# An encoder layer on one core: GpSimd left idle until the routing, and the last normalisation rebuilt around PSUM

## The chip, the cores and the metric

One core of a Trainium2 chip runs the kernel. The metric is the device time of one execution in microseconds (us). TensorE is called PE, VectorE DVE, ScalarE ACT, GpSimd POOL; SP is the engine that here only issues transfers.

## The reference, cut to what matters

```python
mod = silu(c) @ w_ada + b_ada                        # 6 vectors: shift, scale, gate, twice
u = x * (1 + sc_a) + sh_a
x = layer_norm(ALPHA * x + g_a * attention_mixer(u), ln1_g, ln1_b)
u = x * (1 + sc_f) + sh_f
x = layer_norm(ALPHA * x + g_f * expert_choice_ffn(u), ln2_g, ln2_b)

def layer_norm(x, g, b):
    mu = mean(x); var = mean((x - mu) ** 2)
    return (x - mu) * rsqrt(var + 1e-5) * g + b

def expert_choice_ffn(u):                            # 16 experts, each takes its 64 best of 512 tokens
    g, idx = top_k(softmax(u @ w_router).T, 64)
    h = silu(u[idx] @ w_gate) * (u[idx] @ w_up)
    return scatter_add((h @ w_down) * g)
```

There are 512 tokens of width 1024, all in f32. The mixer holds 8 heads of latent attention and 4 heads of differential attention; the experts are 2048 wide, so that their weights are 16 x 3 x 8 MB.

## The kernel before

The **front** (about the first 325 us) computes the conditioning vectors, the projections and both attentions, in 32 steps `s`: 16 units of differential attention, then 16 of latent attention. Fillers (projections, latents, their normalisation, the splits below) are woven into the steps. Most products run as three products of a rounded part and a remainder: `split` has ACT write the rounded part and another engine subtract it to get the remainder (line L237). Before, POOL does this subtraction for the normalised latents, the queries and half of `w_ukv`, and in `wo_split` both the multiplication of a block of `w_out` by the gate row (L734) and its subtraction. `wo_split` of the first four blocks stands at steps `W0 + i * WD` = 9, 12, 15, 18; their products (`ga`) begin at step 20. `lat_sums` holds the Newton chain for the norm of the latents (L624 to L168 on the tile `small`); the transposes at L631 wait for it. In this part a scheduler sets the order of the instructions on each engine, from a model of their durations.

The **experts** run in 8 pairs. SP streams the weights through 1 MB pages in a fixed order (`stream`, issued in `prefetch` at L954 whenever a page is free): 16 pages of `w_gate`, 16 of `w_up`, 16 of `w_down` for a pair. In the last pair the second half of `w_down` comes in half pages, first those of output columns 0 to 511 (c = 0), then those of 512 to 1023 (c = 1). `up` multiplies block by block, k = 0 to 7; the last blocks of `w_up` are taken column by column, so that `hidden` (DVE) and `hidden_t` (transposes, L1353) of one column run beside the next.

The **last pair** ends in `down_last`. After each block of c = 1 `finish_first` brings one tile's columns 0 to 511 home: a product that scatters (PE), an addition and the statistics (DVE). `gated(1)` scales the other half, four products scatter it into four banks that hold the residual already (by a product with the identity), and `finish` normalises. It runs two Newton chains on DVE, one for two tiles each, and shares multiplications and additions out to DVE, ACT and POOL. The last norm's weight and bias come as one row (`last_rows`), which `spread` copies to all partitions by products of one row with ones (PE, then ACT and DVE empty the banks).

From the routing to the end the order is the program's own (`manual_schedule`).

Of the kernel before, what the change touches and what calls it, by code (L numbers as in the profile page):

```python
# [11 lines left out]
I32 = mybir.dt.int32  # L12
# [4 lines left out]
P = 128  # L17
# [1 line left out]
D = 1024  # L19
KB = 8  # L20
KEEP = 2
W0, WD = 9, 3
MODS = (1, 2, 3, 4, 5, 6, 7, 8, 9)
NEXP = 16
FF = 2048
# [77 lines left out]
def encoder_layer(ctx: ExitStack, tc: tile.TileContext, xT, x, wadaT, cvec, colp, rowp, rows, cst, pos, posr,  # L103
# [503 lines left out]
    def lat_evac(j, bank):  # L607
        hc, c = pages.get(2)
        hs, s = pages.get(2)
        copy(ACT, c, bank)  # L610
        ACT.activation(s, bank, AF.Square)
        lat[j] = (hc, c, hs, s)
        if j == 1:
            POOL.tensor_tensor(s, s, lat[0][3], op=OP.add)

    def lat_sums(bank):
        one = csb[:, C_ONE:C_ONE + 1]
# [17 lines left out]
    def lat_norm(j, bank):  # L635
        hc, c = lat[j][0], lat[j][1]
        DVE.scalar_tensor_tensor(c, c, cols[:, V_GQ + j:V_GQ + j + 1], bank, op0=OP.mult, op1=OP.mult)
        LN_[j] = split(c, 512, POOL)
        pages.put(hc)

    WK, WQ = {}, {}
# [1 line left out]
    def wk_load():  # L643
        hr, raw = pages.get(4)
        SP.dma_start(raw, w_ukv)
        WK["kh"], WK["k"] = split(raw[:, :512], 512, DVE)
        WK["vh"], WK["v"] = split(raw[:, 512:], 512, POOL)
        pages.put(hr)

    def wq_load(p):  # L650
# [51 lines left out]
    def q_proj(h, bank):  # L702
        hw, w = WQ[h // 2]
        for j in range(2):
            o = j * 256 + (h % 2) * P
            mm3(bank, w[:, o:o + P], LN_[j][1][:, :], j == 0, j == 1)
        if h % 2:
            pages.put(hw)
        hf, f = pages.get(2)
        DVE.tensor_tensor(f, bank, CSQ[h % 2], op=OP.mult)  # L710
        QM[h] = split(f, 512, DVE if h < 0 else POOL)
        pages.put(hf)


# [16 lines left out]

    def wo_split(k):
        hr, raw = WO[k]
        POOL.tensor_tensor(raw, raw, GR["r"], op=OP.mult)  # L734
        WOh[k], WO[k] = split(raw, 1024, POOL)
        pages.put(hr)

    Zh, Z = [], []
# [561 lines left out]
    def last_rows():  # L1300
# [3 lines left out]

    late = {(0, "g", 5): take_xs, (0, "g", 6): take_gate, (0, "g", 7): take_hidden, (0, "u", 4): take_hidden_t,
            (0, "u", 5): take_rows, (0, "d", 2): lambda: take_acc(0), (0, "d", 4): lambda: take_acc(1),
            (1, "g", 0): lambda: pages.put(EP["gbh"]), (NP - 1, "g", 7): last_rows}

    def turn(pr, nm, k, hs):
        put_all(hs)  # L1310
# [5 lines left out]
    def up(pr, nm, banks, between, columns=None):  # L1316
# [4 lines left out]
                r = slice(64 * e, 64 * e + 64)  # L1321
                PE.matmul(banks[c][r], xs[:, k, r], w[e][:, c * 512:(c + 1) * 512], start=k == 0, stop=k == 7)  # L1322

        n = KB if columns is None else KB - 2
        for k in range(n):
            h, w = zip(*(loaded.pop((pr, nm, k, e)) for e in range(2)))
            between(k)
# [62 lines left out]

    LB, TB, YB = HALF[0], HALF[1][:2], HALF[1][2:]

    def finish_first(t):
        scatter(NP - 1, t, 0, TB[t % 2])
        DVE.bn_stats(lst[:, 24 * t:24 * t + 6], acc[t][:, 0:512])

    def finish():
        crit.close()
        with tc.manual_schedule():
            gated(1, YB)  # L1400
            for t in range(4):
                mm(LB[t], OHT[(NP - 1) % 2][:, t * P:(t + 1) * P], EP["YS"][:, 512:], False, True)
            l2 = EP["l2"]
            m2 = mv2[:, 0:8].rearrange("p (t c) -> p t c", c=2)
            va, t1, rs, nb = (lst[:, 20 + 24 * j:24 + 24 * j] for j in range(4))

            def half(t, c):
                src = LB[t] if c else acc[t][:, :512]
                return src, acc[t][:, c * 512:(c + 1) * 512], l2[:, c * 512:(c + 1) * 512], l2[:, D + c * 512:D + (c + 1) * 512]

            def stats(t):
                return [lambda: DVE.bn_stats(lst[:, 24 * t + 6:24 * t + 12], LB[t]),  # L1412
                        lambda: DVE.bn_aggr(mv2[:, 2 * t:2 * t + 2],
                                            lst[:, 24 * t:24 * t + 12].rearrange("p (c s) -> p c s", s=6))]

            def centre(t, c):
                src, a, g, b = half(t, c)
                return lambda: DVE.scalar_tensor_tensor(a, src, mv2[:, 2 * t:2 * t + 1], g, op0=OP.subtract, op1=OP.mult)  # L1418

            def store(t, c):  # L1420
                SP.dma_start(out[t * P:(t + 1) * P, c * 512:(c + 1) * 512], acc[t][:, c * 512:(c + 1) * 512])

            def scaled(t, c):
                src, a, g, b = half(t, c)

                def go():
                    DVE.scalar_tensor_tensor(a, a, rs[:, t:t + 1], b, op0=OP.mult, op1=OP.add)  # L1427
                    store(t, c)
                return go

            def other(t, c, last=POOL):
                src, a, g, b = half(t, c)
                ACT.activation(a, src, AF.Identity, scale=rs[:, t:t + 1], bias=nb[:, t:t + 1])
                POOL.tensor_tensor(a, a, g, op=OP.mult)
                last.tensor_tensor(a, a, b, op=OP.add)

            def newton(t):
                p = slice(t, t + 2)
                return [lambda: DVE.tensor_scalar(va[:, p], m2[:, p, 1], LN_EPS, RS_SCALE, op0=OP.add, op1=OP.mult)] + \
                    rsqrt_steps(rs[:, p], va[:, p], t1[:, p], mv2[:, 8 + t:10 + t].bitcast(I32)) + \  # L1440
                    [lambda: DVE.scalar_tensor_tensor(nb[:, p], m2[:, p, 0], -1.0, rs[:, p], op0=OP.mult, op1=OP.mult)]

            def weave(steps, work):
                for i, step in enumerate(steps):
                    step()
                    if i % 2 and work:
                        work.pop(0)()
                for w in work:
                    w()

            for f in stats(0) + stats(1):
                f()
            weave(newton(0), stats(2) + stats(3) + [centre(0, 0), centre(1, 0)])
            other(0, 1)
            other(1, 1)
            weave(newton(2), [scaled(0, 0), scaled(1, 0), centre(2, 0), centre(2, 1), centre(3, 0)])
            store(0, 1)
            scaled(2, 0)()
            scaled(2, 1)()
            store(1, 1)  # L1460
            scaled(3, 0)()
            other(3, 1, DVE)
            store(3, 1)

    for pr in range(NP):
        G, U = HALF[pr % 2], HALF[1 - pr % 2]

        def in_gate(k, pr=pr, U=U):
            if pr == 0:
                gather(0, U[2:], (k + 2) * (k > 0), min(k + 3, KB))  # L1470
                if k == KB - 1:
                    scat_mats(0, U[2])
            elif 1 <= k <= 4:
                for hf in range(2):
                    scatter(pr - 1, k - 1, hf, U[hf])
# [110 lines left out]
```

## Time and profile before

| | |
|---|---|
| time, median of 3 runs (lowest to highest) | 1303.66 us (1299.6 to 1304.99) |
| the profiled execution | 1303.92 us, its span 1302.1 us |
| busy in the span | PE 1185.2, DVE 373.8, ACT 225.0, POOL 118.7 us |
| mean granted clock of PE | 0.969 |
| moved by DMA | 456.10 MB, mean 350 GB/s |

The span runs from the first to the last instruction; 1.8 us of the time lie outside it. A row of a timeline gives start, duration, engine, line, operation, what is written and read, the shape and the count; brackets hold the idle time of the engine ahead of it and what ended that. A granted clock of 1.00 is 2.4 GHz, 0.50 is 1.2 GHz.

### The profile page before, as it was taken

How to read it: one execution, taken by the hardware profiler on the slowest of the kernel's cores; microseconds unless marked ns; L12 is line 12 of the kernel's file. 1: busy time of each engine (PE TensorE's matmuls, PEld its weight loads, DVE VectorE, ACT ScalarE, POOL GpSimd, SP SyncE). 2: the span in 40 equal slices, each digit the busy share in tenths (PEclk: the TensorE clock that was granted, in tenths of full speed). 3: DMA queues.
4: the chain of work that ended last, by engine and by line, in shares of the span. 5: the costliest groups of instructions: out<-in, count | busy, mean ns of one | idle time of the engine just before them, and what ended most of it. 6: DMA issues, size and time to landing. Idle time of an engine off the chain costs nothing.

```text
span 1302.1 us, 13908 instructions
## 1 busy us (share of the span) xinstructions
PE 1185.2 (91%) x5581; PEld 550.5 (42%) x5581; DVE 373.8 (29%) x793; ACT 225.0 (17%) x464; POOL 118.7 (9%) x79
## 2 busy tenths in 40 slices
PE   8899888999899999998899799879978997998793
PEld 5677556777433433432342243224323432432231
DVE  6798897636301111020110012010101110110107
ACT  3465665542210000000000000000000000000000
POOL 2500532320000500000000000000000000000002
PEclk9899998999999999999999999999998999999987
DMA  9775531374999899999999999999999999999981
GB/s 345 291 231 194 176 138 65 130 283 154 385 385 420 335 422 421 421 421 421 421 422 421 421 422 421 421 421 421 422 421 421 420 421 422 421 422 421 422 304 65
DMA packets 76215, 456.10 MB, mean 350 GB/s; under 512 B 8140, under 2 KB 8524, under 8 KB 28018
## 3 DMA queue, kind: packets, MB, share of 16 engines
q1 hardware_dynamic: 75858, 455.08, 86.3%
q8 instruction: 44, 0.72, 0.2%
q14 instruction: 23, 0.19, 0.0%
q10 hardware_dynamic: 290, 0.10, 0.0%
HBM read 453.04 MB, written 3.95 MB: 351 GB/s over the span
## 4 chain that ended last, share of the span: by engine, by line
DMA 45%; PE 27%; DVE 2%; issue 0%; ACT 0%; SPq 0%; DVEq 0%
DMA pg<-in_w_up_dram 19%; DMA pg<-in_w_gate_dram 15%; PE bk L122 14%; PE bk L1322 11%; DMA pg<-in_w_down_dram 11%; PE bk L1353 1%; DVE pg L1427 0%; DVE pg L1418 0%; DVE small L1192 0%; DVE ohg L1194 0%; DVE lst L1412 0%; DVE lst L162 0%; PE bk L1243 0%; DVE mv L165 0%; PE bk L1271 0%
## 5 line engine op out<-in xcount | busy, mean ns | idle before, releaser
L122 PE MATMUL bk<-pg,pg 128*128 128x512 f32 (+4 forms) x2282 | 530.9, 490 | 13.6 <-POOL pg L423 4.4
L122 PEld LDWEIGHTS bk<-pg,pg 128*64 128x64 f32 (+2 forms) x2282 | 259.7, 163 | 237.5 <-issue 176.3
L1322 PE MATMUL bk<-pg,pg 128*64 128x512 f32 x1024 | 242.8, 609 | 35.1 <-DMA pg<-in_w_up_dram 33.6
L1322 PE MATMUL bk<-pg,xs 128*64 128x512 f32 x1024 | 241.0, 605 | 30.3 <-DMA pg<-in_w_up_dram 30.0
L1322 PEld LDWEIGHTS bk<-pg,pg 128*64 128x64 f32 x1024 | 73.6, 139 | 193.3 <-issue 128.5
L1322 PEld LDWEIGHTS bk<-pg,xs 128*64 128x64 f32 x1024 | 73.3, 138 | 183.0 <-issue 124.3
L1347 DVE TENSOR_TENSOR pg<-pg,bk 128x512 f32<-128x512 f32 x32 | 22.0, 688 | 405.0 <-PE bk L1322 405.0
L144 ACT ACTIVATE pg<-bk 128x512 f32<-128x512 f32 (+1 forms) x105 | 59.3, 583 | 434.2 <-PE bk L1353 353.7
L1226 POOL TENSOR_TENSOR ohg<-ohg,aff 128x512 f32<-128x512 f32 x8 | 8.4, 1049 | 789.5 <-DVE ohg L1225 789.5
L1249 DVE TENSOR_TENSOR pg<-pg,bk 128x512 f32<-128x512 f32 x60 | 41.3, 688 | 124.7 <-PE bk L122 124.4
L122 PEld LDWEIGHTS bk<-ohg,pg 128*128 128x128 f32 x512 | 61.3, 196 | 28.8 <-issue 28.8
L122 PE MATMUL bk<-ohg,pg 128*128 128x128 f32 x512 | 67.9, 286 | 0.5 <-DVE ohg L1225 0.5
L1343 ACT ACTIVATE pg<-bk 128x512 f32<-128x512 f32 x32 | 18.8, 598 | 241.3 <-PE bk L1322 241.3
L137 ACT ACTIVATE pg<-pg 128x512 fp32r<-128x512 f32 (+2 forms) x63 | 42.8, 708 | 26.0 <-DVE pg L710 7.0
L237 POOL TENSOR_TENSOR pg<-pg,pg 128x512 fp32r<-128x512 f32 (+1 forms) x20 | 34.8, 1745 | 91.6 <-ACT pg L137 91.5
L1008 DVE CUSTOM_DVE_ANT_0 pg<-pg,pg 128x1024 f32<-128x1024 f32 x32 | 39.7, 1276 | 2.3 <-DMA pg<-in_wadaT_dram 2.2
L1238 DVE TENSOR_SCALAR xs<-bk,Gc,Bc 128x128 f32<-128x128 f32 x16 | 6.6, 410 | 100.1 <-PE bk L122 100.1
L1238 DVE TENSOR_SCALAR pg<-bk,Gc,Bc 128x128 f32<-128x128 f32 x16 | 6.6, 410 | 97.7 <-PE bk L122 97.7
L122 PE MATMUL bk<-pg 64*128 64x512 f32 (+3 forms) x94 | 30.5, 485 | 3.2 <-DMA pg<-in_cvec_dram 2.2
L1386 DVE TENSOR_TENSOR pg<-bk,pg 128x512 f32<-128x512 f32 x16 | 11.1, 692 | 67.5 <-PE bk L122 67.5
L1353 PEld LDWEIGHTS bk<-csb,pg 128*128 128x128 f32 x128 | 17.8, 209 | 26.1 <-issue 22.8
L218 DVE CUSTOM_DVE_ANT_0 pg<-pg,pg 128x1024 f32<-128x1024 f32 x16 | 25.7, 1640 | 5.7 <-DMA pg<-in_wadaT_dram 5.7
(211 smaller groups left out, 629.4 us busy)
## 6 DMA issues: line engine op xcount, KB each, us to landing
pg<-in_w_gate_dram SPq DMA_DIRECT2D x128, 1024.0 KB, 19.8
pg<-in_w_up_dram SPq DMA_DIRECT2D x128, 1024.0 KB, 19.8
pg<-in_w_down_dram SPq DMA_DIRECT2D x120, 1024.0 KB, 19.8
pg<-in_wadaT_dram SPq DMA_DIRECT2D x16, 1024.0 KB, 7.3
pg<-in_wadaT_dram SPq DMA_DIRECT2D x16, 512.0 KB, 6.2
pg<-in_w_down_dram SPq DMA_DIRECT2D x16, 512.0 KB, 10.8
pg<-bias_d SPq DMA_DIRECT2D x16, 256.0 KB, 4.8
pg<-in_w_out_dram SPq DMA_DIRECT2D x8, 512.0 KB, 3.2
```

The source lines that it names most:

```text
L122: PE.matmul(o, l, r, start=start, stop=stop)
L137: return ACT.activation(dst, src, AF.Copy, scale=scale)
L144: ACT.activation(dst, src, AF.Copy)
L218: DVE.tensor_tensor_reduce(out=w2[:, j], in0=w2[:, j], in1=cs, scale=1.0, scalar=0.0, op0=OP.mult, op1=OP.add, accum_out=modr[:, n:n + 1])
L237: lo_eng.tensor_tensor(lo, src, ff(hi), op=OP.subtract)
L1008: DVE.tensor_tensor_reduce(out=w2[:, j], in0=w2[:, j], in1=cs, scale=1.0, scalar=0.0, op0=OP.mult, op1=OP.add, accum_out=modr[:, n:n + 1])
L1238: DVE.tensor_scalar(xs[:, k, :], src, Gc[:, k:k + 1], Bc[:, k:k + 1], op0=OP.mult, op1=OP.add)
L1249: DVE.tensor_add(acc[t][:, c], acc[t][:, c], bank)
L1322: PE.matmul(banks[c][r], xs[:, k, r], w[e][:, c * 512:(c + 1) * 512], start=k == 0, stop=k == 7)
L1343: ACT.activation(EP["HS"][:, c * 512:(c + 1) * 512], banks[c], AF.Silu)
L1347: DVE.tensor_tensor(s, s, U[c], op=OP.mult)
L1353: PE.transpose(G[c % 2][:, i * P:(i + 1) * P], sj[:, i // 2, i % 2, :], ident)
```

## The change

1. In the front every subtraction and multiplication that POOL did from the latents on (`lat_evac`, `lat_norm`, `wk_load`, `q_proj`, `wo_split`) goes to DVE: 13 instructions of 512 elements for each partition and 16 of 1024. `W0, WD` go from 9, 3 to 15, 1.
2. In `up` only k = 7 is taken column by column, in all pairs; before it was k = 6 and 7.
3. `last_rows` takes its page and issues its transfer one gate stage earlier, and `spread` runs in the last pair's gate stage (ahead of k = 6) and no longer after block 1 of its down stage.
4. `finish_first` multiplies a tile's first half by the norm's weight right after its statistics. `finish` runs one Newton chain for all four tiles. The first half of three tiles is made in PSUM: the identity times the bias, a diagonal matrix of -mean/deviation times the weight, and a diagonal matrix of 1/deviation times the weighted values, which ACT then copies out. The second halves and the last tile's first half end on DVE. POOL has nothing left in it.

```diff
-W0, WD = 9, 3
+W0, WD = 15, 1
...
         if j == 1:
-            POOL.tensor_tensor(s, s, lat[0][3], op=OP.add)
+            DVE.tensor_tensor(s, s, lat[0][3], op=OP.add)
...
-        LN_[j] = split(c, 512, POOL)
+        LN_[j] = split(c, 512, DVE)
...
-        WK["vh"], WK["v"] = split(raw[:, 512:], 512, POOL)
+        WK["vh"], WK["v"] = split(raw[:, 512:], 512, DVE)
...
-        QM[h] = split(f, 512, DVE if h < 0 else POOL)
+        QM[h] = split(f, 512, DVE)
...
-        POOL.tensor_tensor(raw, raw, GR["r"], op=OP.mult)
-        WOh[k], WO[k] = split(raw, 1024, POOL)
+        DVE.tensor_tensor(raw, raw, GR["r"], op=OP.mult)
+        WOh[k], WO[k] = split(raw, 1024, DVE)
...
-            (1, "g", 0): lambda: pages.put(EP["gbh"]), (NP - 1, "g", 7): last_rows}
+            (1, "g", 0): lambda: pages.put(EP["gbh"]), (NP - 2, "d", KB - 1): last_rows}
...
-        n = KB if columns is None else KB - 2
+        n = KB if columns is None else KB - 1
...
     def finish_first(t):
         scatter(NP - 1, t, 0, TB[t % 2])
-        DVE.bn_stats(lst[:, 24 * t:24 * t + 6], acc[t][:, 0:512])
+        a = acc[t][:, :512]
+        DVE.bn_stats(lst[:, 24 * t:24 * t + 6], a)
+        DVE.tensor_tensor(a, a, EP["l2"][:, :512], op=OP.mult)
...
+        bias(0)
+        gated(1, YB)
+        bias(1)
+        for t in range(4):
+            mm(LB[t], OHT[(NP - 1) % 2][:, t * P:(t + 1) * P], EP["YS"][:, 512:], False, True)
+            DVE.bn_stats(lst[:, 24 * t + 6:24 * t + 12], LB[t])
+            DVE.bn_aggr(mv2[:, 2 * t:2 * t + 2], lst[:, 24 * t:24 * t + 12].rearrange("p (c s) -> p c s", s=6))
+        bias(2)
+        bias(3)
+        DVE.tensor_scalar(va, m2[:, :, 1], LN_EPS, RS_SCALE, op0=OP.add, op1=OP.mult)
+        rsqrt(rs, va, t1, mv2[:, 8:12].bitcast(I32))
+        DVE.scalar_tensor_tensor(nb, m2[:, :, 0], -1.0, rs, op0=OP.mult, op1=OP.mult)
+
+        for t in range(4):
+            ACT.activation(diag[:, t], ident, AF.Copy, scale=nb[:, t:t + 1])
+            mm(banks[t], diag[:, t], l2[:, :512], False, t == 3)
+            if t < 3:
+                ACT.activation(diag[:, 4 + t], ident, AF.Copy, scale=rs[:, t:t + 1])
+                mm(banks[t], diag[:, 4 + t], acc[t][:, :512], False, True)
+        for t in range(4):
+            centre(t)
+            scaled(t)
+            if t < 3:
+                ACT.activation(acc[t][:, :512], banks[t], AF.Copy)
+            else:
+                a = acc[t][:, :512]
+                DVE.scalar_tensor_tensor(a, a, rs[:, t:t + 1], banks[t], op0=OP.mult, op1=OP.add)
+            store(t, 0)
...
             elif 1 <= k <= 4:
                 for hf in range(2):
                     scatter(pr - 1, k - 1, hf, U[hf])
+            elif k == 6 and pr == NP - 1:
+                spread(EP["l2"], U[2:], (1.0, 1.0))
...
             if pr == NP - 1:
-                if b == 1:
-                    spread(EP["l2"], TB, (1.0, 1.0))
                 if b >= 2:
```

Here `bias(t)` is the product of the identity with the bias half row into `banks[t]`, `centre` is (value - mean) times the weight from the bank, and `scaled` is that times 1/deviation plus the bias, with the store behind it.

**Order on DVE in the front.** Before, the end of the Newton chain for the latents (tile `small`, 128x8) stands among the softmax instructions of differential attention (L527 reads a score bank `bk`, L537 to L539 combine its two maps):

```order
L166 SCALAR_TENSOR_TENSOR small<-small 128x8
L539 SCALAR_TENSOR_TENSOR pg_129_3057<-pg_129_3057,st 128x512
L162 TENSOR_TENSOR small<-small 128x8
L527 ISA pg_7_110,st<-bk_68,pg_34_271 128x512
L527 ISA st 128x1
L537 RECIPROCAL st<-sts 128x1
L162 TENSOR_TENSOR small<-small 128x8
L538 SCALAR_TENSOR_TENSOR st<-sts,small,st 128x1
L167 SCALAR_TENSOR_TENSOR small<-small 128x8
L539 SCALAR_TENSOR_TENSOR pg_142_3124<-pg_142_3124,st 128x512
L168 SCALAR_TENSOR_TENSOR small<-small 128x8
```

Now the same end of the chain has only small instructions in it:

```order
L166 SCALAR_TENSOR_TENSOR small<-small 128x8
L162 TENSOR_TENSOR small<-small 128x8 x2
L167 SCALAR_TENSOR_TENSOR small<-small 128x8
L537 RECIPROCAL st<-sts 128x1
L168 SCALAR_TENSOR_TENSOR small<-small 128x8
```

A little later in the changed kernel the gate multiplications of `w_out` (L734) and their subtraction (L237) stand between the softmax instructions on DVE, where there was nothing of them:

```order
L527 ISA pg_1_78,st<-bk_67,pg_34_271 128x512
L527 ISA st 128x1
L734 TENSOR_TENSOR pg_206_3446<-pg_206_3446,pg_41_314 128x1024
L537 RECIPROCAL st<-sts 128x1
L167 SCALAR_TENSOR_TENSOR st<-st 128x4
L481 SCALAR_TENSOR_TENSOR pg_144_3178<-bk_69,pg_144_3178 128x512
L527 ISA pg_1_78,st<-bk_68,pg_34_271 128x512
L527 ISA st 128x1
L734 TENSOR_TENSOR pg_212_3478<-pg_212_3478,pg_41_314 128x1024
L538 SCALAR_TENSOR_TENSOR st<-sts,small,st 128x1
L168 SCALAR_TENSOR_TENSOR st<-st 128x4
L237 TENSOR_TENSOR pg_210_3475<-pg_206_3446,pg_210_3475 128x1024
```

So the chain got shorter by its neighbours, and POOL's work on `w_out` went in behind it, with the later steps in the program notwithstanding: the scheduler places these instructions while differential attention still runs.

**Order on PE at the end of the last pair's up stage.** Before, a column (one bank `bk`) takes four weight pages, those of k = 6 and of k = 7; a row is one product:

```order
L1322 MATMUL bk_66<-pg_1063_7456,pg_385_4750 64x512
L1322 MATMUL bk_66<-pg_1064_7458,pg_385_4750 64x512
L1322 MATMUL bk_66<-pg_1068_7470,pg_385_4750 64x512
L1322 MATMUL bk_66<-pg_1071_7484,pg_385_4750 64x512
L1322 MATMUL bk_67<-pg_1063_7456,pg_385_4750 64x512
L1322 MATMUL bk_67<-pg_1064_7458,pg_385_4750 64x512
L1322 MATMUL bk_67<-pg_1068_7470,pg_385_4750 64x512
L1322 MATMUL bk_67<-pg_1071_7484,pg_385_4750 64x512
L1353 MATMUL bk_70<-csb,pg_393_4787 128x128 x4
```

Now k = 6 (pages 1060 and 1063) is through all four banks before the first product that needs k = 7:

```order
L1322 MATMUL bk_68<-pg_1060_7462,pg_381_4746 64x512
L1322 MATMUL bk_68<-pg_1063_7472,pg_381_4746 64x512
L1322 MATMUL bk_69<-pg_1060_7462,pg_381_4746 64x512
L1322 MATMUL bk_69<-pg_1063_7472,pg_381_4746 64x512
L1322 MATMUL bk_66<-pg_1064_7474,pg_381_4746 64x512
L1322 MATMUL bk_66<-pg_1067_7488,pg_381_4746 64x512
L1322 MATMUL bk_67<-pg_1064_7474,pg_381_4746 64x512
L1322 MATMUL bk_67<-pg_1067_7488,pg_381_4746 64x512
L1353 MATMUL bk_70<-csb,pg_389_4783 128x128 x4
```

Six products of k = 6 (columns 1 to 3) moved from behind the arrival of k = 7 to ahead of it.

## Rows read from the trace of the kernel before

**Rows 1.** Stages, by stretch: PE, PEld, DVE, ACT, POOL busy; PEclk; DMA share; GB/s.
```profile
125.00:150.00 25.00, 20.22 (x125) 15.88 (x124) 24.03 (x60) 13.56 (x36) 11.20 (x5) 0.98 0.55 189
150.00:212.00 62.00, 52.39 (x280) 36.68 (x280) 52.59 (x124) 39.29 (x91) 19.29 (x11) 0.93 0.36 125
212.00:290.00 78.00, 76.59 (x518) 59.54 (x516) 42.15 (x71) 41.41 (x91) 25.20 (x12) 0.98 0.47 178
...
455.00:1186.00 731.00, 675.94 (x3030) 249.32 (x3028) 84.06 (x134) 36.40 (x67) 6.30 (x6) 0.99 1.01 421
1186.00:1224.00 38.00, 28.38 (x114) 8.53 (x108) 0.00 (x0) 2.05 (x4) 0.00 (x0) 0.96 1.01 421
```

**Rows 2.** PE timeline of the last pair, from the last weights of the up stage.
```profile
1224.75 4.15 PE L1322 MATMUL bk<-pg,pg 128*64 128x512 f32 x10 [1.42 <-DMA pg<-in_w_up_dram]
...
1234.60 3.65 PE L122 MATMUL bk<-pg,pg 128*64 128x512 f32 x16
...
1242.44 5.29 PE L122 MATMUL bk<-pg,csb 1*128 1x512 f32 x8
1247.66 5.50 PE L122 MATMUL bk<-pg,pg 128*64 128x512 f32 x16
1253.09 1.98 PE L122 MATMUL bk<-pg,csb 128*128 128x512 f32 x4
...
1260.50 22.07 PE L122 MATMUL bk<-pg,pg 128*64 128x512 f32 x80
```

**Rows 3.** Issues of w_down from 1224.5 us on (first and last start), and time to landing.
```profile
L954 SPq DMA_DIRECT2D pg<-in_w_down_dram x17: 327/541/3215, 1224.8 to 1255.5; - x17
...
DMA to landing us min/median/max: 10.4/10.8/19.9
```

**Rows 4.** DVE timeline of the end of the kernel.
```profile
1278.12 0.69 DVE L1386 TENSOR_TENSOR pg<-bk,pg 128x512 f32<-128x512 f32 x1 [0.46 <-PE bk L122]
...
1281.21 0.21 DVE L1413 BATCH_NORM_AGGREGATE mv<-lst 128x2 f32<-128x12 f32 x1
...
1285.06 0.75 DVE L1418 SCALAR_TENSOR_TENSOR pg<-pg,mv,pg 128x512 f32<-128x512 f32 x1
...
1298.34 0.68 DVE L1435 TENSOR_TENSOR pg<-pg,pg 128x512 f32<-128x512 f32 x1
```

**Rows 5.** Waits of PE from 95 to 330 us, the longest.
```profile
PE bk L631 <- DVE small L168: 4.0, 1, 4.0
```

**Rows 6.** POOL's instructions from 90 to 330 us, grouped by line.
```profile
L237 POOL TENSOR_TENSOR pg<-pg,pg 128x512 fp32r<-128x512 f32 (+1 forms) x20 | 34.8, 1745 | 91.6 <-ACT pg L137 91.5
L734 POOL TENSOR_TENSOR pg<-pg,pg 128x1024 f32<-128x1024 f32 x8 | 21.0, 2635 | 11.6 <-DMA pg<-in_w_out_dram 10.3 <-ACT pg L144 1.3
L614 POOL TENSOR_TENSOR pg<-pg,pg 128x512 f32<-128x512 f32 x1 | 1.3, 1283 | 34.4 <-ACT pg L611 34.4
```

**Rows 7.** DVE timeline of the front.
```profile
122.61 1.35 DVE L162 TENSOR_TENSOR st<-st 128x4 f32<-128x4 f32 x2
...
135.65 0.16 DVE L162 TENSOR_TENSOR small<-small 128x8 f32<-128x8 f32 x1
...
138.38 0.74 DVE L539 SCALAR_TENSOR_TENSOR pg<-pg,st 128x512 f32<-128x512 f32 x1
139.04 2.35 DVE L162 TENSOR_TENSOR small<-small 128x8 f32<-128x8 f32 x1
...
142.00 1.76 DVE L162 TENSOR_TENSOR small<-small 128x8 f32<-128x8 f32 x1
...
143.93 2.87 DVE L539 SCALAR_TENSOR_TENSOR pg<-pg,st 128x512 f32<-128x512 f32 x1
146.72 2.30 DVE L168 SCALAR_TENSOR_TENSOR small<-small 128x8 f32<-128x8 f32 x1
...
208.79 2.20 DVE L571 SCALAR_TENSOR_TENSOR pg<-pg,st,rowb 128x128 f32<-128x128 f32 x4
...
214.34 1.22 DVE L1008 CUSTOM_DVE_ANT_0 pg<-pg,pg 128x1024 f32<-128x1024 f32 x1
```

More of the change, by code (lines that the diff above doesn't have):

```diff
@@ L1394, in finish_first @@
         scatter(NP - 1, t, 0, TB[t % 2])
-        DVE.bn_stats(lst[:, 24 * t:24 * t + 6], acc[t][:, 0:512])
+        a = acc[t][:, :512]
+        DVE.bn_stats(lst[:, 24 * t:24 * t + 6], a)
+        DVE.tensor_tensor(a, a, EP["l2"][:, :512], op=OP.mult)
     def finish():
-        crit.close()
[L1399 to L1463, printed above, removed]
@@ new lines, in finish, with bias, store, centre @@
+        l2, diag = EP["l2"], EP["HS"].rearrange("p (i q) -> p i q", q=P)
+        banks = [YB[0], TB[0], TB[1], YB[1]]
+        m2 = mv2[:, 0:8].rearrange("p (t c) -> p t c", c=2)
+        va, t1, rs, nb = (lst[:, 20 + 24 * j:24 + 24 * j] for j in range(4))
+        def bias(t):
+            mm(banks[t], ident, l2[:, D:D + 512], True, False)
+        def store(t, c):
+            SP.dma_start(out[t * P:(t + 1) * P, c * 512:(c + 1) * 512], acc[t][:, c * 512:(c + 1) * 512])
+        def centre(t):
+            DVE.scalar_tensor_tensor(acc[t][:, 512:], LB[t], mv2[:, 2 * t:2 * t + 1], l2[:, 512:D], op0=OP.subtract, op1=OP.mult)
@@ new lines, in scaled @@
+        def scaled(t):
+            a = acc[t][:, 512:]
+            DVE.scalar_tensor_tensor(a, a, rs[:, t:t + 1], l2[:, D + 512:], op0=OP.mult, op1=OP.add)
+            store(t, 1)
+        bias(0)
[5 more added lines that the diff above has]
+            DVE.bn_aggr(mv2[:, 2 * t:2 * t + 2], lst[:, 24 * t:24 * t + 12].rearrange("p (c s) -> p c s", s=6))
```

## The prediction

> **What bounds the kernel now.** I read the stages first [rows 1]. From 455 us to the last pair the DMA share is 1.01 at 421 GB/s: the stream of expert weights has no gap and sets the pace, while PE has slack (675.9 of 731 us). Nothing in the change makes the stream smaller, so only two places can give time: what comes before the stream runs without a gap, and what comes after its last weights. In the front PE should be the bound; it is busy for 76.59 of 78 us from 212 to 290, but only for 20.22 of 25 and 52.39 of 62 before that. There DVE is busy for 24.03 of 25 and 52.59 of 62: differential attention is bound by DVE. A time gained or lost in the front passes through whole, since PE starts the experts and the pages come free from there.
>
> The end is the second view: the timeline of PE in the last pair [rows 2]. From 1224.75 on PE is the bound. The reader should see three things. The up stage still has 10 product halves to do when its last weights arrive, at half the pace (4.15 us for 10, where 16 take 3.65), and more behind them. Then a block of 8, the copying of a row to all partitions, takes 5.29 us, and the 16 after it 5.50. And from 1260.50 all is back to back. Meanwhile the weights have arrived: the last transfer is issued at 1255.5 and lands 10.4 us later, at 1265.9 [rows 3], but the last product ends only at 1278.0, just ahead of `gated(1)` at 1278.12 [rows 4]. PE is 12 us behind the stream here.
>
> **The change, part by part.** The sum is made against the profiled execution, 1303.9 us with a span of 1302.1 (the median shown is 1303.7, so the difference carries over).
>
> *k = 7 alone by columns.* When the last page of `w_up` arrives, PE now has 14 halves left in place of 26. The 12 that went ahead (the order on PE shows them as six products) fill its wait for that page. At 3.65/16 = 0.23 us each that is 2.7 us [rows 2]. PE also ran at half clock after its idle wait: 10 halves took 4.15 in place of 2.3, so 1.9 more if it stays busy there. Bounds 2.7 and 4.6; I take 4.0, because the wait is filled mostly. In the other pairs the stream covers it.
>
> *Spread moved.* 5.29 us leave PE's path, and the clock loss behind them, 5.50 - 3.65 = 1.85 us, goes too [rows 2]: 7.1. It now costs about the same in the gate stage, where PE has 38.00 - 28.38 = 9.6 us of idle time to come before the last page [rows 1]. That covers it; without the cover it would be 7.1 us, less what the weights' arrival allows.
>
> *What is late next.* 4.0 + 7.1 = 11.1 us earlier, PE meets the weights. Block 3 of the down stage has its last page at 1224.8 + 19.9 = 1244.7 [rows 3]. From there PE needs 14 halves of block 3 (3.2), two products with the identity (1.98), 64 halves of c = 0 and 1 (14.6) and three scatter products (half of 1.98 each, 3.0): 1267.5. By the other bound the last page lands at 1265.9 and 8 halves (1.8) follow: 1267.7. Both say that the last product ends at about 1268.0 in place of 1278.0. This term is **-10.0**; it would be -11.1 without the weights, and -6 if PE dropped to half clock for some 8 us while it waits for half pages.
>
> *The tail.* Before, from 1278.0 to the end of the last DVE instruction (1298.34 + 0.68) are 21.0 us, and 3.1 more to the end of the span [rows 4]. Now, from the last product on: the fourth scatter 1.0 (two halves); on DVE addition, statistics and the new multiplication ahead of `gated(1)`, 3 x 0.69 = 2.1; `gated(1)` 0.7; the first product of the other half 1.0; four times statistics and aggregate, 4 x (0.61 + 0.21) = 3.3 (0.69 less the 0.08 by which DVE starts the next one early); eleven small instructions, each 0.16 (a row follows in the front's part) and 0.2 from start to start, 2.2; a diagonal on ACT, 0.3 (an estimate, a quarter of a bank copy with its fixed part); seven products on PE at 1.0, 6.9; the last DVE instruction 0.75; 3.1 as before; and about 0.1 for each of eight changes of engine. Sum 22.2 against 24.1. DVE's own eight instructions at 0.7 (5.6 us) lie beside the products. If the products run at half clock, 6.9 becomes 13.8; PE is idle for about 2 us ahead of them. I take half a step of that kind, 1 us. This term is **-1.0**, bounds -3 and +5.
>
> *The front.* PE's longest wait there is for the Newton chain of the latents, 4.0 us [rows 5]. POOL is busy for 34.8 + 21.0 + 1.3 us in this part [rows 6]. While it runs, some DVE instructions are stretched: a small one of the chain takes 2.35 or 1.76 us in place of 0.16, another 2.30, a combination 2.87 in place of 0.74 [rows 7]. The stretched ones read two operands from SBUF. There are 11 such rows between 122.61 and 208.79, and over all of them the excess is 16.2 us. With POOL silent I expect it gone. Against that stands the added work. Until the eighth row maximum of latent attention (about 212 us before) 9 instructions of 512 and 9 of 1024 elements stand newly on DVE; issued back to back they cost about 0.61 and 1.14 (a row shows 1.22, and the next starts some 0.08 before its end), 15.7 us together. So DVE's load up to there stays as it was, within 1 us. What changes is where the lost time lies: 8.0 us of the stretch were inside the chain, for which PE waited 4.0. The order on DVE shows the chain now short and the work on `w_out` behind it. After 212 DVE has 42.15 of 78 us busy [rows 1]; the rest of the 28 us, some 12, fits in. I take **-3.0**: the wait goes, a little is lost elsewhere. Bounds: -14.4, all of PE's idle time from 125 to 212; and +15.7, if nothing is given back.
>
> [...]
>
> The row's page, taken one gate stage earlier, leaves the stream one page less for some 20 transfers; with 19.9 us from issue to landing at 2.5 us a page the queue is eight deep, so one less costs nothing.
>
> Sum: 1303.9 - 10.0 - 1.0 - 3.0 = 1289.9. I predict **1290 us**.
>
> **The rivals.**
> (a) *The front gains nothing or loses a little.* The scheduler's new order puts 1.2 us instructions between the softmax ones, and each may hold a bank that PE wants. For it: DVE is 96% busy from 125 to 150 [rows 1]. Against it: the stretched rows [rows 7]. With +3 in place of -3: 1296.
> (b) *The diagonal products run at half clock.* For it: PE is idle before them, and the row after the spread shows what that does. Against: the pause is short. 6.9 more, with 1 already in: 1296.
> (c) *DVE becomes the front's bound* (the other side). The stretch is not POOL's doing, so nothing comes back: +15.7 until 212, and of the 12 us after that half reach PE's path, since its softmax waits for the same engine: +21.7 in place of -3. 1303.9 - 11.0 + 21.7 = 1314.6. It decides once the front loses more than 11 us. Against it: rows of the same line, with and without POOL beside them, differ by 2 us.
> (d) *The spread isn't covered in its new place.* PE enters the last pair's up columns late, and 3 to 4 us of the term of 10 are lost: 1293.5.
> (e) *The end does nothing*: with PE earlier, the half pages come later, since their issue hangs on something else. Then only -4 stay: 1300. Against it: the last issue at 1255.5 follows landings, not PE.
>
> **How the numbers follow.** Chances: forecast 0.52, (a) 0.17, (b) 0.09, (c) 0.07, (d) 0.10, (e) 0.05. A measurement can tell about 0.5% from no change, that is below 1297.1 or above 1310.2. Faster are the forecast, (b) and (d) and 60% of (a): 0.81. Slower is (c): 0.07. The rest, 0.12, is the same. The forecast's own range is 1285 to 1294. To leave out no more than 2 in 10, the range goes from 1282 (a front that gives 8 us more) to 1299 (above (a), (b) and (d), short of (e)).
>
> **What would show it.** In the profile after: the wait of L631 for L168 gone, no stretched DVE rows, PE's idle time from 125 to 212 below 14.4; in the last pair no row of one-row products behind block 1, waits of PE for `w_down` pages, and the last product within 3 us of the last landing, not 12; in the tail no POOL, and seven products at 0.43 a half. Wrong would make it: a DVE that is busy throughout the front while PE's waits grow, or diagonal products at 0.86 a half.

## The result, and the profile after

The changed kernel takes 1282.59 us (median of 4 runs, 1282.34 to 1285.97) against 1304.02 for the kernel before on the same chip: a ratio of 0.9848, with a 95% interval from 0.982 to 0.9876. Differences between two changed kernels, below, are of their medians; taken by the ratios to the kernel before they come out the same within 1.3 us. The intervals are 2 to 4 us wide to either side, so that a smaller difference is not clear of the noise by the times alone, and the traces have to bear it. The change makes the kernel faster, by 21 us where 14 were forecast. The profiled execution took 1282.34 us, its span is 1280.5 us (1302.1 before).

I split the 21.6 us by events that both traces have: the start of the first product of the experts (`L1322`) and the landing of the last page of `w_down`. First the instructions of `L1322` in the kernel before, by kind (first and last start within the stretch asked for):

```profile
L1322 PE MATMUL bk<-pg,xs x30: 592/592/644, 342.7 to 350.0; 128*64 128x512 f32 x30
```

The same in the changed kernel:

```profile
L1322 PE MATMUL bk<-pg,xs x64: 592/592/643, 332.5 to 349.6; 128*64 128x512 f32 x64
```

And its last transfers of `w_down` with their time to landing, which answer to [rows 3]:

```profile
L954 SPq DMA_DIRECT2D pg<-in_w_down_dram x16: 539/606/3242, 1215.0 to 1243.7; - x16
...
DMA to landing us min/median/max: 10.5/10.8/15.2
```

| | before | after | difference | predicted |
|---|---|---|---|---|
| start to first product of the experts | 342.7 | 332.5 | -10.2 | -3.0 |
| from there to the last landing | 923.3 | 921.7 | -1.6 | 0 |
| from there to the end of the last product | 12.0 | 2.9 | -9.1 | -10.0 |
| from there to the end of the span | 24.1 | 23.4 | -0.7 | -1.0 |

(The last landing is at 1254.2, 10.5 us behind the issue at 1243.7.)

**The front.** The stages of the changed kernel, with the columns of [rows 1]; the second runs to the ninth row maximum of latent attention, which is taken up further below:

```profile
125.00:150.00 25.00, 25.00 (x151) 18.15 (x150) 22.27 (x75) 15.97 (x39) 0.00 (x0) 1.00 0.52 164
...
125.00:199.79 74.79, 68.57 (x405) 50.19 (x404) 69.97 (x187) 53.02 (x123) 0.00 (x0) 0.98 0.49 169
...
212.00:290.00 78.00, 76.75 (x543) 60.16 (x542) 43.98 (x79) 40.88 (x91) 0.00 (x0) 1.00 0.46 172
...
412.00:422.00 10.00, 10.00 (x51) 6.42 (x50) 1.51 (x3) 1.05 (x2) 9.30 (x4) 0.83 0.92 371
```

PE has no pause from 125 to 150, where it had 4.78 us, and POOL is silent. The longest waits of PE from 95 to 330 us (total, times, longest), which answer to [rows 5]:

```profile
PE bk L122 <- DVE pg L710: 4.3, 2, 3.9
PE bk L122 <- ACT pg L137: 3.3, 2, 2.6
```

The wait of L631 is gone; the longest is now for a query's multiplication (L710), ahead of 199.8 us, and the second for ACT's roundings, behind it. The end of the Newton chain for the latents in the DVE timeline, where [rows 7] have 2.35, 1.76 and 2.30 us:

```profile
129.60 0.16 DVE L162 TENSOR_TENSOR small<-small 128x8 f32<-128x8 f32 x1
...
131.32 0.37 DVE L162 TENSOR_TENSOR small<-small 128x8 f32<-128x8 f32 x2
...
132.11 0.15 DVE L168 SCALAR_TENSOR_TENSOR small<-small 128x8 f32<-128x8 f32 x1
...
132.49 0.75 DVE L539 SCALAR_TENSOR_TENSOR pg<-pg,st 128x512 f32<-128x512 f32 x1
...
199.79 0.68 DVE L870 TENSOR_REDUCE st<-bk 128x1 f32<-128x512 f32 x1
```

No row from 80 to 300 us is stretched any more. The last line is the ninth row maximum of latent attention; before, it starts at 212.34.

**The last pair.** PE's timeline, which answers to [rows 2]:

```profile
1212.48 1.93 PE L1322 MATMUL bk<-pg,pg 128*64 128x512 f32 x6 [1.33 <-DMA pg<-in_w_up_dram]
...
1227.92 3.65 PE L122 MATMUL bk<-pg,pg 128*64 128x512 f32 x14 [0.70 <-DMA pg<-in_w_down_dram]
...
1238.91 19.26 PE L122 MATMUL bk<-pg,pg 128*64 128x512 f32 x72
...
1261.01 3.70 PE L122 MATMUL bk<-pg,pg 128*128 128x512 f32 x8 [1.12 <-DVE pg L1386]
...
1268.37 7.97 PE L122 MATMUL bk<-pg,pg 128*128 128x512 f32 x14 [1.94 <-ACT pg L1434]
```

The one-row products are gone from here, and PE now waits for a page of `w_down` (0.70): it has caught up with the stream. The 72 halves end at 1258.17 with the fourth scatter, so the last product ends about 1.0 earlier, at 1257.1. The last line holds the seven diagonal products in 14 halves; 14 at full clock take 6.28 us (a later row), so the clock fell within them (granted 0.79 over these 7.97 us). DVE's timeline of the end, which answers to [rows 4]:

```profile
1259.66 0.69 DVE L1398 TENSOR_TENSOR pg<-pg,pg 128x512 f32<-128x512 f32 x1
1260.27 0.68 DVE L1386 TENSOR_TENSOR pg<-bk,pg 128x512 f32<-128x512 f32 x1
1262.17 0.70 DVE L1425 BATCH_NORM_STATS2 lst<-bk 128x6 f32<-128x512 f32 x1 [1.22 <-PE bk L122]
...
1267.71 0.16 DVE L1431 SCALAR_TENSOR_TENSOR lst<-mv,lst 128x4 f32<-128x4 f32 x1
...
1276.38 0.75 DVE L1446 SCALAR_TENSOR_TENSOR pg<-pg,lst,bk 128x512 f32<-128x512 f32 x1 [2.71 <-PE bk L122]
```

`gated(1)` (L1386) stands behind 2.1 us of other work, PE waits for it, and at the end DVE waits 2.71 us for the diagonal products.

### The profile page after: what moved, and what is told of

It reads as the page before. It is cut to its first block, busy times and chain, and to the rows that moved or that the text cites. A ratio compares the mean times of both kernels' runs of the same rounds, so it can differ in the third digit from the quotient of the medians.

```text
span 1280.5 us, 13903 instructions
## 1 busy us (share of the span) xinstructions
PE 1181.4 (92%) x5603; PEld 554.0 (43%) x5603; DVE 375.4 (29%) x813; ACT 228.2 (18%) x471; POOL 53.9 (4%) x45
## 4 chain that ended last, share of the span: by engine, by line
PE 37%; DMA 36%; DVE 2%; issue 0%; ACT 0%; SPq 0%; DVEq 0%
PE bk L122 23%; DMA pg<-in_w_up_dram 19%; PE bk L1322 13%; DMA pg<-in_w_down_dram 9%; DMA pg<-in_w_gate_dram 8%; PE bk L1353 0%; PE bk L1243 0%; DVE small L1192 0%; DVE ohg L1194 0%; DVE lst L1425 0%; PE bk L1271 0%; DVE mv L1426 0%; DVE pg L1446 0%; DVE lst L1397 0%; ACT aff L838 0%
## 5 line engine op out<-in xcount | busy, mean ns | idle before, releaser
L122 PE MATMUL bk<-pg,pg 128*128 128x512 f32 (+4 forms) x2296 | 542.2, 488 | 22.9 <-ACT pg L137 7.1
L122 PEld LDWEIGHTS bk<-pg,pg 128*128 128x128 f32 (+2 forms) x2296 | 263.1, 161 | 253.6 <-issue 177.5
L1322 PE MATMUL bk<-pg,pg 128*64 128x512 f32 x1024 | 236.4, 601 | 33.4 <-DMA pg<-in_w_up_dram 28.9
L1322 PE MATMUL bk<-pg,xs 128*64 128x512 f32 x1024 | 234.3, 598 | 29.9 <-DMA pg<-in_w_up_dram 27.2
L1322 PEld LDWEIGHTS bk<-pg,pg 128*64 128x64 f32 x1024 | 73.7, 137 | 185.0 <-issue 124.1
L1322 PEld LDWEIGHTS bk<-pg,xs 128*64 128x64 f32 x1024 | 72.7, 136 | 176.5 <-issue 118.8
L1343 ACT ACTIVATE pg<-bk 128x512 f32<-128x512 f32 x32 | 18.8, 598 | 222.1 <-PE bk L1322 222.1
L137 ACT ACTIVATE pg<-pg 128x512 fp32r<-128x512 f32 (+2 forms) x63 | 42.4, 707 | 21.3 <-DVE pg L896 5.2
L237 DVE TENSOR_TENSOR pg<-pg,pg 128x512 fp32r<-128x512 f32 (+1 forms) x40 | 37.1, 933 | 14.8 <-ACT pg L137 14.6
L1008 DVE CUSTOM_DVE_ANT_0 pg<-pg,pg 128x1024 f32<-128x1024 f32 x32 | 37.9, 1221 | 2.1 <-DMA pg<-in_wadaT_dram 2.0
L1386 DVE TENSOR_TENSOR pg<-bk,pg 128x512 f32<-128x512 f32 x16 | 11.1, 691 | 74.7 <-PE bk L122 74.7
L1353 PEld LDWEIGHTS bk<-csb,pg 128*128 128x128 f32 x128 | 17.8, 209 | 26.5 <-DVE pg L1347 13.5
L218 DVE CUSTOM_DVE_ANT_0 pg<-pg,pg 128x1024 f32<-128x1024 f32 x16 | 24.6, 1574 | 5.7 <-DMA pg<-in_wadaT_dram 5.7
```

The source lines that it names most:

```text
L122: PE.matmul(o, l, r, start=start, stop=stop)
L137: return ACT.activation(dst, src, AF.Copy, scale=scale)
L218: DVE.tensor_tensor_reduce(out=w2[:, j], in0=w2[:, j], in1=cs, scale=1.0, scalar=0.0, op0=OP.mult, op1=OP.add, accum_out=modr[:, n:n + 1])
L237: lo_eng.tensor_tensor(lo, src, ff(hi), op=OP.subtract)
L1008: DVE.tensor_tensor_reduce(out=w2[:, j], in0=w2[:, j], in1=cs, scale=1.0, scalar=0.0, op0=OP.mult, op1=OP.add, accum_out=modr[:, n:n + 1])
L1343: ACT.activation(EP["HS"][:, c * 512:(c + 1) * 512], banks[c], AF.Silu)
```

## The experiments

My theory of the front was that DVE and POOL keep each other from SBUF, so that POOL's silence gives the gain. The rival was that the order gives it: the later steps of `w_out` and the work that the scheduler puts ahead of the chain. Of the end, the theory was the prediction's: PE was late, and the columns and the spread made it so.

**The front alone**: before, with part 1 of the change.

> The kernel before with part 1 alone (POOL's front work to DVE, steps 15, 1); the end is that of before. The trace after shows the first expert product 10.2 us earlier than before, and 9.8 us less from the last landing of weights to the end. If the parts add up, this one gives 10 to 12 us: 1292 to 1294. If the early weights of the front were only needed together with the new end, less than 5: 1299 or more.

Measured: 1294.63 us (1292.86 to 1295.92), ratio 0.994 (0.9918 to 0.9963), 8.3 us less than the kernel before, measured beside it; I had expected 10 to 12. The experts begin at 335.7 us in its trace, 3.2 later than in that of the changed kernel, with the same work (more on that below). The end is as before, 35.75 us from the last landing.

**The end alone**: the changed kernel with the front of before.

> The changed kernel with the front of before (POOL does its subtractions, steps 9, 3), so parts 2 to 4 alone. If the parts add up: 9.5 to 11 us less than before, 1293 to 1295, with the first expert product at 342 to 343 us as before, and about 26 us from the last landing to the end.

Measured: 1291.51 us (1290.46 to 1292.24), ratio 0.9916 (0.9896 to 0.9936), 11.4 us less, just above the 9.5 to 11 that I expected. The two parts add up to 19.7 of the 21 us, so they hardly touch each other. The experts begin at 342.3, and the end takes 24.67 us from the last landing; its 14 halves run at full clock here:

```profile
1279.97 6.28 PE L122 MATMUL bk<-pg,pg 128*128 128x512 f32 x14 [1.94 <-ACT pg L1434]
```

**The old steps** in the changed kernel:

```diff
-W0, WD = 15, 1
+W0, WD = 9, 3
```

> The changed kernel with W0, WD back at 9, 3: the same work on DVE, another order. Theory A (POOL's silence takes the stretch out of DVE's instructions, and that is the gain of the front): 1281 to 1286. Theory B (the new steps and the order that follows from them are the gain): 1288 or more, first expert product 5 us later than in the changed kernel.

Measured: 1286.41 us (1285.45 to 1287.17), ratio 0.9877 (0.9857 to 0.9897), so 3.8 us more than the changed kernel. That lies between the ranges of the two theories. The ninth row maximum comes at 209.8 in place of 199.8, and the experts begin at 338.8, later than in the traces with the new steps, this work on DVE and POOL silent (332.5 to 335.7). So the order has a share, but not the whole.

**The new steps alone**: the kernel before with `W0, WD = 15, 1`, POOL at work as before.

> The kernel before with W0, WD = 15, 1 and nothing else: POOL still does its work. Theory A: within 2 us of before, 1302 to 1306, since POOL's instructions stretch DVE wherever they stand. Theory B: 5 us or more less, below 1299.

Measured: 1300.7 us (1298.23 to 1304.83, 10 runs), ratio 0.9987 (0.9969 to 1.0005). No gain that can be told from none (the median lies between the two ranges that I gave); the experts begin at 343.6, and DVE's stretch is 20.2 us (18.8 before, counted in the same way, as the excess over the median of the unstretched). So the later steps are worth something only where DVE does the work.

**Only the short work, and only the work on `w_out`, to DVE.** The first moves the 13 instructions of 512 elements and keeps 9, 3; the second moves `wo_split` and takes 15, 1.

> The kernel before with only the 13 short instructions on DVE (steps 9, 3); w_out's work stays on POOL, 40 us of 57. Theory A: 12 to 15 us of stretch are left, and the gain is 1 to 4 us: 1299 to 1302. If the short ones matter: 5 us or more, below 1298.

> The kernel before with only w_out's multiplications and subtractions on DVE (steps 15, 1); the 13 short instructions stay on POOL, 17 us of 57. Theory A: most of the stretch is gone, 5 us or less is left of 18.8, and 4 to 8 us are gained: 1295 to 1299. If the short ones, which sit in the chains that PE waits for, are what matters: within 3 us of before.

Measured: the short work gives 1300.72 us (1296.36 to 1302.45, 10 runs), ratio 0.999 (0.9975 to 1.0005), with a stretch of 18.0 us beside 39.0 us of POOL work. The work on `w_out` gives 1296.17 us (1292.06 to 1297.98), ratio 0.9949 (0.9928 to 0.997), with a stretch of 8.5 us beside 18.5 us of POOL work (57.0 before). I had expected less stretch of both, 12 to 15 us and 5 or less. The stretch is nearly all there as long as the work on `w_out` is on POOL, and the time falls only where that is moved. It does not follow the stretch strictly: with only the work on `w_out` moved, the experts begin at 334.4 us, as early as in the changed kernel, although 8.5 us of stretch are left.

**POOL reads again.** The changed kernel, with POOL repeating the subtractions into a tile that nobody reads:

```diff
         lo_eng.tensor_tensor(lo, src, ff(hi), op=OP.subtract)
+        if dup:
+            for o in range(0, n, 512):
+                POOL.tensor_tensor(ohg[:, 512:], src[:, o:o + 512], ff(hi[:, o:o + 512]), op=OP.subtract)
```

> The changed kernel, and POOL repeats the subtraction of 20 of the splits into a tile that nobody reads there (28 instructions of 512 elements, about 36 us of POOL); nothing waits for it but the reuse of pages. Theory A (POOL's reading of SBUF stretches DVE): the stretched DVE rows come back, 8 to 13 us of them, and the time is 1285 to 1291. If POOL's presence as such costs nothing and only the order matters: 1282 to 1284 and no stretched rows.

Measured: 1296.11 us (1293.6 to 1297.78, 7 runs), ratio 0.9956 (0.9942 to 0.9971): 13.5 us more than the changed kernel, above the range that I expected, although the results of POOL are not used. The experts begin at 346.9, which is later than before the change. POOL's group from 110 to 330 us:

```profile
L240 POOL TENSOR_TENSOR ohg<-pg,pg 128x512 f32<-128x512 f32 x28 | 48.8, 1743 | 150.4 <-ACT pg L137 149.0
```

DVE's timeline beside it:

```profile
142.22 0.68 DVE L237 TENSOR_TENSOR pg<-pg,pg 128x512 fp32r<-128x512 f32 x1
142.82 0.68 DVE L530 CUSTOM_DVE_ANT_0 pg<-bk,pg 128x512 f32<-128x512 f32 x1
...
144.55 1.25 DVE L162 TENSOR_TENSOR st<-st 128x4 f32<-128x4 f32 x1
145.73 2.98 DVE L237 TENSOR_TENSOR pg<-pg,pg 128x512 fp32r<-128x512 f32 x3
```

An operation on four elements (L162), 0.16 us elsewhere, takes 1.25; the softmax instruction that reads a bank and one tile keeps its 0.68. DVE's stretch is 17.9 us. The scheduler also gives DVE another order here: of its 612 instructions up to 348 us in the changed kernel 550 keep theirs. What the stretch alone does shows up to the ninth row maximum, at 214.23:

```profile
125.00:214.23 89.23, 76.85 (x418) 55.16 (x416) 84.23 (x196) 54.97 (x128) 28.27 (x16) 0.90 0.44 148
```

DVE is busy for 84.23 us in place of 69.97, and idle for 5.00 in place of 4.82; 12.6 of the 14.3 us more are stretch. This settles the theory for the stretch: it comes with POOL's work beside DVE. Of DVE's instructions that overlap a POOL subtraction here, 19 of the 35 that read two tiles of SBUF are stretched and 1 of the 28 others (L164 at 177.18, with one tile, 1.26 us in place of 0.16); in the kernel before it is 14 of 21 and none of 45. That it is POOL's reading, and not its writing, is argued and not shown: the instructions that I gave to POOL do both. The Trainium skill says so in SBUF — State Buffer, Who interferes with whom: a DVE instruction with two inputs from SBUF contends with a GpSimd instruction that reads SBUF, not with one that only writes it, and the port pair that they share is an exclusive lock. The rows here agree with the part on two inputs, but for L164 and one more such row with one tile in the kernel with the new steps alone.

**The old spread**: the changed kernel with `spread` back behind block 1 of the last down stage.

> The changed kernel with the spread of the last row back behind block 1 of the last pair's down stage. By the prediction's term (5.3 us of PE and 1.9 of half clock behind it, less what the weights' arrival hides): 5 to 7 us more than the changed kernel, 1288 to 1290. If the stream of weights sets the end in any case: within 1.5 us of it.

Measured: 1287.58 us (1282.89 to 1287.85), ratio 0.9886 (0.9861 to 0.9911), 5.0 us more. One of its four runs took 1282.89, no longer than the changed kernel; there is no trace of that one. PE's timeline of a run of 1287.85:

```profile
1228.74 4.91 PE L122 MATMUL bk<-pg,csb 1*128 1x512 f32 x8
1233.58 5.87 PE L122 MATMUL bk<-pg,pg 128*64 128x512 f32 x16
...
1246.80 18.63 PE L122 MATMUL bk<-pg,pg 128*64 128x512 f32 x72
```

The 16 halves behind the one-row products take 5.87 us in place of 3.65 again. The last product ends at 1264.4, 7.9 us behind the last landing (1256.5), where the changed kernel has 2.9.

**The old columns**: the changed kernel with `n = KB if columns is None else KB - 2`.

> The changed kernel with k = 6 and 7 by columns again in the up stage (part 2 undone). By the terms of the prediction: 12 product halves go back behind the last page of w_up, 4.0 us of PE's path less the 1.1 us that the arrival of w_down hid, so 2.9 us more than the changed kernel's 1282.6, 1285.5 (bounds +1.3 and +4: 1283.9 to 1286.6), and the last product ends about 6 us after the last landing in place of 2.9. Rival: the moved spread alone lets PE reach the weights of w_down, the stream hides the columns, and the time stays within 1 us of 1282.6.

Measured: 1286.64 us (1282.36 to 1287.01), ratio 0.988 (0.986 to 0.99). PE's timeline of the profiled execution, which is the one of 1282.36:

```profile
1212.74 4.16 PE L1322 MATMUL bk<-pg,pg 128*64 128x512 f32 x10 [1.42 <-DMA pg<-in_w_up_dram]
...
1241.29 18.63 PE L122 MATMUL bk<-pg,pg 128*64 128x512 f32 x72
...
1270.11 6.28 PE L122 MATMUL bk<-pg,pg 128*128 128x512 f32 x14 [1.94 <-ACT pg L1434]
```

The 72 halves end at 1259.92, 1.75 us later than in the changed kernel with the same landing (1254.2). But the diagonal products keep the full clock and give 1.69 back (6.28 for 7.97), so that the span ends at 1280.6, with no difference. The other three runs are 4 us slower; there is no trace of them, so what the columns cost there stays open.

**The old finish**: the changed kernel with the old `finish_first` and `finish`.

> The changed kernel with the old finish and finish_first (two Newton chains, work on POOL and ACT; part 4 undone). By the prediction's tail term: 1.0 us more than the changed kernel, 1283.6. By the traces: 27.0 us from the last landing to the end of the span (2.9 + 24.1) against 24.65 to 26.4 in the new tails with and without PE's full clock in the diagonal products, so 0.6 to 2.4 us more, 1283.2 to 1285.0. Rival: the new tail is worth nothing once the weights bound the end, 1282.6 within 0.5.

Measured: 1284.71 us (1283.22 to 1287.02), ratio 0.987 (0.9849 to 0.9891), 2.1 us more by the medians and 0.9 more by the profiled executions, neither clear of the noise. It takes 27.0 us from the last landing, as expected. POOL's work stretches DVE here too; three rows of its timeline:

```profile
1268.07 1.76 DVE L1427 SCALAR_TENSOR_TENSOR pg<-pg,lst,pg 128x512 f32<-128x512 f32 x1
1269.75 1.21 DVE L162 TENSOR_TENSOR lst<-lst 128x2 f32<-128x2 f32 x1
...
1271.08 1.76 DVE L1418 SCALAR_TENSOR_TENSOR pg<-pg,mv,pg 128x512 f32<-128x512 f32 x1
```

**`gated(1)` first.** DVE's view of the end shows 2.1 us of work ahead of `gated(1)` that `gated(1)` does not need. This version puts it ahead of them:

```diff
     def scatter(pr, t, hf, bank, ahead=None):
         mm(bank, OHT[pr % 2][:, t * P:(t + 1) * P], EP["YS"][:, c], True, True)
+        if ahead:
+            ahead()
...
-        scatter(NP - 1, t, 0, TB[t % 2])
+        scatter(NP - 1, t, 0, TB[t % 2], None if t < 3 else lambda: gated(1, YB))
```

A further one also ends the third tile's first half on DVE, as the fourth's, with one diagonal product less.

> The changed kernel with gated(1) ahead of the addition, statistics and multiplication of the fourth finish_first on DVE. Theory: the tail is a chain DVE gated(1) -> PE scatter -> DVE statistics -> Newton -> PE diagonal products, so that DVE's 2.1 us of other work leave the path and what takes their place is about 0.4: 1.7 us less, 1280.9. Rival: the statistics of four tiles on DVE (back to back with the moved work) or the diagonal products at half clock set the end, and it stays within 0.7 us of 1282.6.

> As the kernel with gated(1) first, and the first half of the third tile ends on DVE like the fourth's (only the -mean/deviation times weight product in PSUM): one 1/deviation product of PE and one copy of ACT less, one DVE instruction more. Theory: PE's diagonal products end last, so that 0.9 us at full clock to 1.7 at half clock leave it, of which DVE's added 0.75 takes some: 0.3 to 0.9 less than the kernel with gated(1) first, 1280.0 to 1280.6. Rival: DVE's eight instructions already run to the end beside PE, and the added one makes it 0.7 us longer, 1281.6.

Measured: `gated(1)` first gives 1281.83 us (1281.02 to 1283.55), ratio 0.9846 (0.9828 to 0.9864); with the third tile on DVE 1282.4 (1279.21 to 1283.18), ratio 0.9837 (0.9817 to 0.9857). I had expected 1280.9, and 1280.0 to 1280.6. Neither can be told from the changed kernel (0.9848) by its time. By the traces the first one works as the theory said: in DVE's timeline `gated(1)` is at 1259.55, ahead of the fourth addition at 1260.41,

```profile
1259.55 0.68 DVE L1388 TENSOR_TENSOR pg<-bk,pg 128x512 f32<-128x512 f32 x1
1260.41 0.69 DVE L1251 TENSOR_TENSOR pg<-pg,bk 128x512 f32<-128x512 f32 x1 [0.18 <-PE bk L122]
...
1275.49 0.75 DVE L1447 SCALAR_TENSOR_TENSOR pg<-pg,lst,bk 128x512 f32<-128x512 f32 x1 [1.01 <-PE bk L122]
```

and from the end of the fourth scatter (1260.38) to the end of the span (1279.6) are 19.2 us, where the kernel with the old columns, also at full clock, has 20.7: 1.5 of the expected 1.7. Its front came 2.2 us later in this execution (334.7), which hides it. The second has 19.4 us there: no further gain. PE's last product ends at 1275.41, and DVE goes on alone, as the rival said, though at no loss of 0.7:

```profile
1274.59 0.75 DVE L1447 SCALAR_TENSOR_TENSOR pg<-pg,lst,bk 128x512 f32<-128x512 f32 x1 [0.74 <-PE bk L122]
...
1276.71 0.74 DVE L1447 SCALAR_TENSOR_TENSOR pg<-pg,lst,bk 128x512 f32<-128x512 f32 x1
```

## Why the prediction was right, and where it was off

The direction and the mechanisms held, and 1282.6 lies just inside the range, at its low end, though outside the forecast's own 1285 to 1294. The low end was put there for a front that gives 8 us more, and 7.2 more came. The miss of 7.4 us is nearly all that one term.

**The front, -3.0, was -10.2: mis-sized.** The step that failed is "I take -3.0: the wait goes, a little is lost elsewhere". The counts behind it held: up to the ninth row maximum (the prediction calls it the eighth) 9 instructions of 512 and 9 of 1024 elements stand newly on DVE, and the stretch is gone. From their near equality (16.2 and 15.7) I took DVE's load as unchanged and priced only PE's wait of 4.0. But PE also waited for DVE in other places, the next largest in the view of [rows 5]:

```profile
PE bk L577 <- DVE pg L571: 2.7, 1, 2.7
```

The kernel before from 125 us to that maximum, which answers to the row to 199.79 above:

```profile
125.00:212.34 87.34, 72.96 (x404) 52.56 (x402) 76.94 (x183) 53.19 (x129) 30.49 (x16) 0.94 0.42 144
```

PE was idle for 14.38 us there and is now for 6.22, although a new wait of 3.9 has come (L710): 8.2 us less, where I had 4.0 less a loss. The other 4.4 us are busy time of PE for as many products; an estimate from the granted clocks in the two rows (0.06 of 87.34 us against 0.02 of 74.79) puts 3 to 4 of them down to the clock. DVE was busy for 76.94 us and is now for 69.97, and idle for 10.40 and now 4.82. So 7.0 us of load went from this part, though the lengthening by POOL and the added work are about equal: other work moved across its ends (from 118 us on 12 of L571, the normalisation of differential attention, in place of 16 stand ahead of the maximum, and of L1008, the sums for the conditioning vectors, two more ran before 118). And 5.6 us of idle time went, as I read it because PE and ACT, which DVE waits for, no longer wait for its late answers. Of the 12.5 us that are gained there (212.34 to 199.79) 2.3 are lost again on the way to the experts, where PE's largest wait is now for ACT (L137, 3.3 us in two waits). POOL's silence with the old steps is worth 5.1 us (1291.51 to 1286.41). The steps 15, 1 hold 3.8 more on top of it, and nothing that can be told from none without it.

**A part of it is the clock.** Seven kernels with this very front begin the experts at 332.5 to 335.7 us, in the mean at 334.1, and the two with the old front at 342.7 and 342.3. The mean is a gain of 8.4. The three early ones have a granted clock of 1.00 from 125 to 150 us, the four late ones 0.93, as the one with `gated(1)` first (from 50 to 60 us it is 0.83 in the early three and 0.66 in the late four):

```profile
125.00:150.00 25.00, 25.00 (x146) 18.81 (x145) 21.35 (x73) 17.28 (x43) 0.00 (x0) 0.93 0.45 148
```

**The stream, 0, was -1.6.** Until some 100 us after its first product PE bounds the experts, not the stream: from 440 to 455 us before, PE is busy for all of 15.00 us and the DMA share is 0.82. Some 80 us after it, in the same place of the program, the kernels differ in the granted clock: 0.83 in all that have POOL silent in the front, 0.66 or 0.67 in all that don't. The ten us from 79.5 after the first product on, in the kernel before:

```profile
422.20:432.20 10.00, 10.00 (x37) 5.38 (x38) 1.10 (x2) 1.03 (x2) 9.18 (x4) 0.67 0.89 369
```

PE's timeline of it around there:

```profile
419.19 4.83 PE L122 MATMUL bk<-pg,csb 1*128 1x512 f32 x8
423.95 3.78 PE L122 MATMUL bk<-ohg,pg 128*128 128x128 f32 x16
427.67 4.20 PE L122 MATMUL bk<-pg,pg 128*64 128x512 f32 x16
```

The same products in the changed kernel, whose stretch is the last row of its stages above:

```profile
409.08 3.88 PE L122 MATMUL bk<-pg,csb 1*128 1x512 f32 x8
412.90 3.66 PE L122 MATMUL bk<-ohg,pg 128*128 128x128 f32 x16
416.48 3.65 PE L122 MATMUL bk<-pg,pg 128*64 128x512 f32 x16
```

The three rows are 1.62 us shorter, which is the whole difference. Why the clock there follows what POOL did 80 us earlier and more, no run shows.

**The last product, -10.0, was -9.1.** It ends 2.9 us behind the last landing; I had 2.1. Of the missing 0.9 the 72 halves have 0.6: they take 19.26 us, and 18.63 in the kernel with the old columns, where PE comes later. That is no loss of clock (the granted one is 1.00 over the 19.26 us) but a wait for a page, which the weight loads (PEld) show:

```profile
1246.42 0.62 PEld L122 LDWEIGHTS bk<-pg,pg 128*64 128x64 f32 x5 [0.45 <-DMA pg<-in_w_down_dram]
```

Undone alone, the spread costs 5.0 us of the last product's end and the columns 1.75; the terms were 7.1 and 4.0, less 1.1 for the weights. What one of them leaves, the arrival of `w_down` hides in part.

**The tail, -1.0, was -0.7**, and the half step of clock that I put in was needed: with full clock the end takes 1.7 us less (6.28 for 7.97). So rival (b) came true by a quarter of its price. Its reason, PE's pause ahead of them, is not enough: the pause is 1.94 us in the full-clock traces of the end alone and of the old columns too.

**The other rivals.** (a) and (c) are refuted by the fronts above: the stretch is POOL's doing and comes back. (d): PE waits 1.33 us for the last page of `w_up` after the spread, so it was covered. (e): PE waits for `w_down`, and the last issue moved with the stream.

## What to carry to other kernels

Where DVE is the bound and its instructions with two inputs from SBUF are stretched, the work of POOL beside them isn't free: sum the stretch, and compare it with what the moved work takes on DVE; if they are about equal, the move can still gain, because the chains that wait for DVE get shorter too. The 13 short instructions alone took 0.8 us of stretch away, and moving them gained nothing that can be told from none. When a stage at the end of a kernel is sped up, look for what arrives last next, and undo the parts one by one: each was worth less than its own busy time here, where a transfer bounds the end. A difference of 2 or 3 us between two executions can be the granted clock of two short stretches, so compare stages at the same granted clock before a cause is given.

## What the runs showed that I had not expected

POOL's work that nobody waits for costs 13.5 us here, for 28 instructions with 48.8 us on POOL and 17.9 us of stretch on DVE, with the other order on DVE in it. The one-row products go with a lower clock: the 14 traces have 28 blocks of eight of them, and around 26 the granted clock falls from 1.00 to 0.50, while they run or right behind them, without a pause of PE in between (the two others are in the traces of the end alone and of `gated(1)` first). 16 halves behind them take 5.50, 5.87 or, in the first pair of the kernel before, 4.20 us in place of 3.65. And the clock in the tail can differ by 1.7 us with the same code there, as much as an edit gives: the 14 halves take 7.97 us in the changed kernel, and 6.28 in the traces of the end alone, of the old steps and of POOL's copies, which end in the same way. No run shows what decides it.
